# The second product of the up projection in five pairs: matmuls of 512 and 256 columns in place of three of 256

## The chip, the cores and the metric

The kernel runs on one core of one Trainium2 chip, in one launch. The metric is the time of that launch on the device, in microseconds; of several runs the median is taken. TensorE, VectorE, ScalarE and GpSimd are called PE, DVE, ACT and POOL in the rows of the profile; PEld is TensorE's weight load, SP is SyncE, from which most DMAs are issued.

## The reference

One block of a decoder on 512 tokens of 2048 channels in float32: an input projection that feeds two token mixers, an output projection, and a gated MLP with a causal convolution of width 3. The change touches the MLP's up projection alone:

```python
def _conv_ffn(h, w_up, conv_w, conv_b, w_down):
    u = h @ w_up                                   # (512, 2048) @ (2048, 11264)
    up = jnp.pad(u, ((0, 0), (CONV_WIDTH - 1, 0), (0, 0)))
    y = conv_b
    for j in range(CONV_WIDTH):
        y = y + conv_w[j] * up[:, j:j + T]
    val, gate = jnp.split(y, 2, axis=-1)
    return (jax.nn.silu(gate) * val) @ w_down
```

The 11264 columns of w_up are 44 blocks of 128 for the value and 44 for the gate.

## The kernel before, in words

**Precision by splitting.** TensorE multiplies in a short form of float32. To keep the precision, each operand is split in two: a high part (ScalarE casts it, L1387) and a low part (VectorE subtracts the high part from the original, L1388). A product then is three matmuls per block of 128 rows of the weights (mm3, L133 to L137): high weights by high activations, high weights by low activations, low weights by high activations. In the up projection each of them streams 256 columns, that is, half of the tokens, since a Strassen-like scheme works on halves.

**The mixed form.** The output projection's halves (out_half, L1301) use another helper, mm2 (L1216 to L1218). There the high and the low activations lie in one operand of two runs of 256 columns, and one matmul of 512 columns takes high weights by both; it fills the whole of a PSUM bank, one half from each. A second matmul of 256 columns adds low weights by high activations to the first half. Whoever reads the bank has to add its two halves.

**A pair.** The up projection walks over 44 pairs, each of a value block and a gate block (the loop is at L1614). A pair of 2 × 2 quarters of weights times 2 × 2 quarters of activations takes seven products instead of eight. Each product has eight weight blocks (8 × 128 rows), so 24 matmuls in mm3's form. In the order of the program these are: w11·Y11 into bank pa (copied to cap by ScalarE, L1633), the last product of the pair before (w22·T4), **w12·Y21 into bank pb**, then r1·T1, r2·T2, r4·Y22 and r3·T3. The r are sums of weight quarters, made on VectorE (r2 at L1649, r4 at L1657) or by DMAs that add on the way (r1, r3). After the product of w12, VectorE adds the bank to cap and writes the first half of u1 (L1639); u1 goes into the convolution (L1470, L1471) once its second half is there (L1659).

**The order of the work.** order at L1611 mixes pairs 10 to 19 with pairs 0 to 9: place 0 is pair 10, place 1 is pair 0, place 2 is pair 11, and so on up to place 19; places 20 to 43 are pairs 20 to 43. For pairs 0 to 9 the first two products were made earlier (first_two, L1409) and stored. Where each engine's instructions stand is decided by a scheduler when the kernel is built; each engine then runs its own in that order. The split weights (tile uw) have three buffers, so splits run ahead of TensorE by up to two products. Banks come from a pool of eight (L1204), each taken whole even where half of it is used.

Of the kernel before, what the change touches and what calls it, by code (L numbers as in the profile page):

```python
# [16 lines left out]
P = 128  # L17
T = 512
# [7 lines left out]
WC = 512  # L26
NWF = 8
NSLOT = 10
NB = 10
NA = 4  # L30
WARB = 5
# [36 lines left out]
def block_kernel(ctx, tc, a, out, stop=None, dbg=None):  # L68
    nc = tc.nc
    V, S, G, PE = nc.vector, nc.scalar, nc.gpsimd, nc.tensor  # L70
# [62 lines left out]
    def mm3(ps, wh, wl, xh, xl, start, stop, more=False, hold=False):  # L133

        muls = [lambda: PE.matmul(ps, wh, xh, start=start, stop=False, skip_group_check=more),  # L135
                lambda: PE.matmul(ps, wh, xl, start=False, stop=False, skip_group_check=more),  # L136
                lambda: PE.matmul(ps, wl, xh, start=False, stop=stop, skip_group_check=more)]  # L137
        if hold:
            late.extend(muls)
            return None  # L140
        if late:
            ins = muls[0]()
            for m in (late.pop(0), muls[1], late.pop(0), muls[2], late.pop(0)):
                with tc.issue_after(ins.ins):
                    ins = m()
            return ins
        for m in muls:
            ins = m()
        return ins
# [772 lines left out]
    def btile(tag="pb"):  # L922

        return psa.tile([P, 2, T], F32, tag=tag, name=tag)
# [263 lines left out]
    pb, py = btile(), btile("py")  # L1188
# [16 lines left out]
    HT = T // 2  # L1205
    H0, H1 = slice(0, HT), slice(HT, T)
    QW = 4 * P

    def bank():
        return psm.tile([P, T], F32, tag="b", name="b")  # L1210
# [5 lines left out]
    def mm2(ps, wh, wl, x, start, stop):  # L1216
        PE.matmul(ps[:, :].rearrange("p (a b) -> p a b", a=2), wh, x, start=start, stop=False)  # L1217
        PE.matmul(ps[:, 0:HT], wl, x[:, 0, :], start=False, stop=stop)  # L1218

    def wide(name):  # L1220

        return rb.tile([P, 4, HT], F32, tag="wide", name=name, bufs=3)
# [13 lines left out]
    def lay(pool, sizes):  # L1236
        for tag, n in sizes:
            pool.tile([P, n], F32, tag=tag, name="lay")
# [87 lines left out]
    Y11, Y21 = [None, None], [None, None]  # L1326
# [33 lines left out]
    ub = ctx.enter_context(tc.tile_pool(name="ub", bufs=1, side="right", reuse_waits="tile"))  # L1360
    lay(ub, [(f"s{i}", T) for i in range(NSLOT)])
    lay(ub, [(f"{t}{g}", 4 * T) for g in range(2) for t in ("t1", "t2", "t3", "y22")])
    lay(ub, [("w2", WS), ("edge", 72)])
    free += [(ub, f"s{i}") for i in range(NSLOT)]

# [15 lines left out]
    def wsplit(src, off=0):  # L1381
        n = src.shape[-1]
        i = nsplit[0] % 3
        nsplit[0] += 1
        w = (ea, ea, ub)[i].tile([P, WS], F32R, tag=f"w{i}", name="uw")
        hi, lo = w[:, off : off + n], w[:, 2 * QW + off : 2 * QW + off + n]
        S.copy(hi, src)  # L1387
        lo_of[0] = V.tensor_tensor(lo, src, hi.bitcast(F32), op=ALU.subtract)  # L1388
        return hi, lo

    def product(ps, w, Y, start=True):
        wh, wl = wsplit(w, 16)
        n = w.shape[-1] // P
        for k in range(n):
            sl = slice(k * P, (k + 1) * P)
            y = Y[k // 4]
            mm3(ps, wh[:, sl], wl[:, sl], y[:, 0, k % 4, :], y[:, 1, k % 4, :], start=start and k == 0,
                stop=k == n - 1, more=not start)

    def row(n, pool, tag):  # L1400
        t = pool.tile([P, 4 * QW], F32, tag=tag, name="wrow")
        nc.sync.dma_start(t, a["wup"][n, :, :])
        return t

    W1, W2 = slice(0, 2 * QW), slice(2 * QW, 4 * QW)
    T1, T2, T3, T4, Y22 = ([None, None] for _ in range(5))
    early = [tc.dram_tile([P, T], F32, name=f"early{n}") for n in range(NB)]

    def first_two(n):  # L1409

        w = row(2 * n, ea, f"t4{n % 2}")
        s_ = Slot("u1")
        ps = bank()[:, 0:HT]
        product(ps, w[:, W1], Y11)
        S.copy(s_[:, H1], ps)
        ps = bank()[:, 0:HT]
        product(ps, w[:, W2], Y21)
        V.tensor_add(s_[:, H0], s_[:, H1], ps)
        G.dma_start(early[n], s_.t)
        s_.done()  # L1420
# [3 lines left out]
    def combos():  # L1424
        for g in range(2):
            normed(g, H1, rstd)
            yield
            t = wide("t1")
            V.tensor_sub(t, x2q[g][:, :, H0], x2q[g][:, :, H1])
            T1[g] = split4(ub, f"t1{g}", t)  # L1430
            yield
            normed(g + 2, H1, rstd)
            yield
            t3 = wide("t3")
            V.tensor_sub(t3, x2q[g + 2][:, :, H1], x2q[g][:, :, H1])
            t2 = wide("t2")
            V.scalar_tensor_tensor(t2, t3, -1.0, x2q[g][:, :, H0], op0=ALU.mult, op1=ALU.subtract)
            yield
            T2[g] = split4(ub, f"t2{g}", t2)
            T3[g] = split4(ub, f"t3{g}", t3)  # L1440
            yield
            Y22[g] = split4(ub, f"y22{g}", x2q[g + 2][:, :, H1])
            V.scalar_tensor_tensor(t2, t2, -1.0, x2q[g + 2][:, :, H0], op0=ALU.mult, op1=ALU.subtract)
            t4.append(t2)
            yield

    steps = combos()
    for n in range(NB):
        first_two(n)
# [142 lines left out]
    def ahead_of_down(j):  # L1592
        if j == NF - 1:
            i = len(A1) // 2
            A1.extend(act_pair(i, *FIRST[i]))
# [3 lines left out]
    def last_product(p):  # L1599

        j, u1, u2, b, w22, x = p
        product(b, w22, T4, start=False)
        if x is None:
            S.copy(u2[:, H0], b)
        else:
            V.tensor_add(u2[:, H0], x[:, H0], b)
            x.done()
        finish_pair(j, u1, u2)


    order = [j for n in range(NB) for j in (NB + n, n)] + list(range(2 * NB, NF))  # L1611

    wq = [rb.tile([P, 4 * QW], F32, tag=f"x2_{i}", name="wquart") for i in (0, 2, 1, 3)]
    for n, j in enumerate(order):  # L1614
        wa, wb = wq[2 * (n % 2)], wq[2 * (n % 2) + 1]

        r1, w11, w12, w22 = wa[:, W1], wa[:, W2], wb[:, W1], wb[:, W2]
        nc.sync.dma_start(r1, a["wup"][2 * j + 1, :, W1])
        G.dma_start(r1, a["wup"][2 * j + 1, :, W2], accum_op=ALU.add)
        nc.sync.dma_start(w11, a["wup"][2 * j, :, W1])  # L1620
        nc.sync.dma_start(w12, a["wup"][2 * j, :, W2])
        nc.sync.dma_start(w22, a["wup"][2 * j + 1, :, W2])
        r3 = wide("r3").rearrange("p a b -> p (a b)")
        nc.sync.dma_start(r3, a["wup"][2 * j, :, W1])
        G.dma_start(r3, a["wup"][2 * j + 1, :, W1], accum_op=ALU.add)
        pa = bank()[:, 0:HT]
        cap = Slot("cap")
        if j < NB:
            u1 = Slot("u1")
            nc.sync.dma_start(u1.t, early[j])  # L1630
        else:
            product(pa, w11, Y11)
            S.copy(cap[:, H0], pa)  # L1633
            if pend:
                last_product(pend)
            u1 = Slot("u1")
            pb = bank()[:, 0:HT]
            product(pb, w12, Y21)
            V.tensor_add(u1[:, H0], cap[:, H0], pb)  # L1639
        ahead_of_down(j)  # L1640
        u2 = Slot("u2")
        pc = bank()[:, 0:HT]
        product(pc, r1, T1)
        S.copy(cap[:, H1], pc)
        if j < NB:
            last_product(pend)
        ahead_of_down(j)
        r2 = wide("r2").rearrange("p a b -> p (a b)")
        V.tensor_add(r2, r1, w11)  # L1649
        product(pa, r2, T2, start=j < NB)  # L1650
        if j < NB:
            V.tensor_add(cap[:, H0], u1[:, H1], pa)
        else:
            S.copy(cap[:, H0], pa)
        ahead_of_down(j)
        r4 = wide("r4").rearrange("p a b -> p (a b)")
        V.tensor_add(r4, r2, w12)  # L1657
        product(pc, r4, Y22, start=False)
        V.tensor_add(u1[:, H1], cap[:, H0], pc)  # L1659
        ahead_of_down(j)  # L1660
        if j < NB:
            pd = bank()[:, 0:HT]
            product(pd, r3, T3)
            V.tensor_add(u2[:, H1], cap[:, H0], cap[:, H1])
            V.tensor_add(u2[:, H1], u2[:, H1], pd)
            pend = (j, u1, u2, pd, w22, cap)
        else:
            product(pa, r3, T3, start=False)
            V.tensor_add(u2[:, H1], cap[:, H1], pa)
            cap.done()  # L1670
            pend = (j, u1, u2, pa, w22, None)
# [194 lines left out]
    for f in range(NWF):  # L1866
# [5 lines left out]
        ps = pss[f] if f < 4 else bank()  # L1872
# [11 lines left out]
    for f in range(NWF, KT):  # L1884
        n = f - NWF
# [107 lines left out]
```

## Time and profile before

| | |
|---|---|
| runs of the kernel before | 2160.95, 2161.58, 2162.29 us; median 2161.58 |
| the profiled execution | 2162.7 us, of which the span from the first to the last instruction is 2160.9 |
| mean granted TensorE clock | 0.992 of full speed |
| busy in the span | PE 98%, PEld 86%, DVE 78%, ACT 48%, POOL 11% |
| matmuls | 17864, with as many weight loads |
| up projection's pairs, 880.2 to 1650 us | PE 769.80 of 769.80 us, DVE 633.67, ACT 427.62, DMA share 0.82 |

A row of the view of instructions in order of time reads: start in us from the span's start, length in us, engine, line of the kernel, operation, what is written and read, shape, count, and in brackets the idle time before it and who ended it. Matmuls are pipelined: a recorded length of 0.28 us is the time through the pipeline, and the next matmul starts before that, so the cost of a matmul in a stream is the distance between two starts. A row of a stage's window gives, for each engine, the time in which it was busy and the number of instructions. In the groups of instructions the last columns are busy us, mean ns of one, and the engine's idle time just before them.

### The profile page before, as it was taken

The numbers are of one execution on the slowest core, as the hardware profiler recorded it, in microseconds if no ns is written. First come the engines' busy times: TensorE is split into PE (matmuls) and PEld (weight loads), VectorE is DVE, ScalarE is ACT, GpSimd is POOL, SyncE is SP. The second block draws the span as 40 slices with busy tenths as digits, with TensorE's granted clock in tenths as the row PEclk, the third lists the DMA queues.
The fourth block names the chain that finished last, engine by engine and source line by source line (L and its number), as shares of the span: only waits on it lengthen the run. The fifth ranks groups of instructions, "written<-read, shape, count | busy, mean of one in ns | idle before, by whom it ended". The sixth has DMA issues, their size and how long they took to land.

```text
span 2160.9 us, 44013 instructions
## 1 busy us (share of the span) xinstructions
PE 2110.9 (98%) x17864; PEld 1866.0 (86%) x17864; DVE 1678.0 (78%) x2615; ACT 1047.8 (48%) x1510; POOL 237.0 (11%) x376
## 2 busy tenths in 40 slices
PE   7999999999999999999999999999999999999997
PEld 3567777777767888999999999999999889987897
DVE  7998898988853678888888887777788657768764
ACT  4354444433433466555555555555556444443353
POOL 0002122221100101110110000000000000120000
PEclk9999999999999999999999999999999999999998
DMA  9976676656537565989888877777777635598764
GB/s 395 393 229 197 200 199 174 199 170 186 150 105 263 183 197 176 290 241 260 253 241 255 236 209 205 207 208 210 209 209 219 211 118 144 161 318 311 243 195 167
DMA packets 169485, 471.89 MB, mean 218 GB/s; under 512 B 21361, under 2 KB 29505, under 8 KB 159169
## 3 DMA queue, kind: packets, MB, share of 16 engines
q1 hardware_dynamic: 120370, 352.12, 48.1%
q0 software_dynamic: 27696, 79.20, 17.5%
q10 hardware_dynamic: 21216, 37.76, 5.7%
q8 instruction: 140, 2.29, 0.4%
q14 instruction: 63, 0.52, 0.1%
HBM read 432.81 MB, written 36.18 MB: 217 GB/s over the span
## 4 chain that ended last, share of the span: by engine, by line
PE 86%; DMA 5%; DVE 4%; ACT 2%; issue 2%; POOL 1%; POOLq 0%; ACTq 0%; DVEq 0%; SPq 0%
PE b L137 19%; PE b L135 19%; PE b L136 19%; PE mm L645 11%; PE pf L426 4%; PE b L1217 2%; PE b L1218 1%; DMA wrow<-wup 1%; PE pb L1047 1%; DVE war L764 1%; DMA wraw<-wout 1%; DMA wa<-ada 1%; PE pa L711 0%; ACT x L1317 0%; DMA wraw<-win 0%
## 5 line engine op out<-in xcount | busy, mean ns | idle before, releaser
L137 PE MATMUL b<-t,uw 128*128 128x256 f32 x1408 | 388.6, 276 | 0.0
L135 PE MATMUL b<-t,uw 128*128 128x256 f32 x1408 | 388.6, 276 | 0.0
L136 PE MATMUL b<-t,uw 128*128 128x256 f32 x1408 | 388.6, 276 | 0.0
L135 PE MATMUL b<-y,uw 128*128 128x256 f32 x1056 | 293.6, 278 | 4.1 <-ACT uw L1387 4.1
L137 PE MATMUL b<-y,uw 128*128 128x256 f32 x1056 | 292.8, 278 | 0.8 <-DVE uw L1388 0.7
L136 PE MATMUL b<-y,uw 128*128 128x256 f32 x1056 | 292.9, 277 | 0.0
L645 PE MATMUL mm<-ahl,whi 128*128 128x512 f32 x864 | 289.7, 409 | 2.1 <-DVE rk L548 1.4
L135 PEld LDWEIGHTS b<-t,uw 128*128 128x128 f32 x1408 | 264.3, 188 | 0.0
L136 PEld LDWEIGHTS b<-t,uw 128*128 128x128 f32 x1408 | 264.3, 188 | 0.0
L137 PEld LDWEIGHTS b<-t,uw 128*128 128x128 f32 x1408 | 264.3, 188 | 0.0
L1388 DVE TENSOR_TENSOR uw<-r,uw 128x1024 fp32r<-128x1024 f32 x164 | 200.6, 1224 | 76.7 <-ACT uw L1387 76.7
L1388 DVE TENSOR_TENSOR uw<-wquart,uw 128x1024 fp32r<-128x1024 f32 x156 | 190.9, 1224 | 68.0 <-ACT uw L1387 67.0
L1387 ACT CAST uw<-wquart 128x1024 fp32r<-128x1024 f32 x156 | 164.1, 1052 | 88.9 <-PE b L137 66.0
L135 PEld LDWEIGHTS b<-y,uw 128*128 128x128 f32 x1056 | 199.5, 189 | 4.8 <-ACT uw L1387 4.8
L137 PE MATMUL b<-act,uw 128*128 128x256 f32 (+1 forms) x608 | 200.5, 330 | 2.7 <-DVE uw L1388 2.7
L1388 DVE TENSOR_TENSOR uw<-wd,uw 128x1024 fp32r<-128x1024 f32 (+1 forms) x112 | 124.1, 1109 | 101.1 <-ACT uw L1387 100.3
L1387 ACT CAST uw<-r 128x1024 fp32r<-128x1024 f32 x164 | 172.5, 1052 | 60.6 <-PE b L137 60.6
L135 PE MATMUL b<-act,uw 128*128 128x256 f32 (+1 forms) x608 | 200.7, 330 | 0.0
L137 PEld LDWEIGHTS b<-y,uw 128*128 128x128 f32 x1056 | 199.5, 189 | 1.2 <-DVE uw L1388 1.2
L136 PE MATMUL b<-act,uw 128*128 128x256 f32 (+1 forms) x608 | 200.4, 330 | 0.0
L136 PEld LDWEIGHTS b<-y,uw 128*128 128x128 f32 x1056 | 199.6, 189 | 0.1
L645 PEld LDWEIGHTS mm<-ahl,whi 128*128 128x128 f32 x864 | 158.2, 188 | 43.2 <-issue 12.2
(356 smaller groups left out, 4601.2 us busy)
## 6 DMA issues: line engine op xcount, KB each, us to landing
wquart<-wup SPq DMA_DIRECT2D x176, 512.0 KB, 5.2
wa<-ada SPq DMA_DIRECT2D x48, 1024.0 KB, 9.1
war<-ada SPq DMA_DIRECT2D x192, 256.0 KB, 3.8
wd<-wdn SPq DMA_DIRECT2D x64, 512.0 KB, 4.1
wraw<-win ACTq DMA_DIRECT2D x118, 256.0 KB, 4.1
wraw<-wout SPq DMA_DIRECT2D x96, 256.0 KB, 3.5
wquart<-wup POOLq DMA_DIRECT2D x44, 512.0 KB, 6.8
r<-wup SPq DMA_DIRECT2D x44, 512.0 KB, 4.7
```

Of the source, the lines that this page charges most:

```text
L135: muls = [lambda: PE.matmul(ps, wh, xh, start=start, stop=False, skip_group_check=more), lambda: PE.matmul(ps, wh, xl, start=False, stop=F ...
L136: lambda: PE.matmul(ps, wh, xl, start=False, stop=False, skip_group_check=more),
L137: lambda: PE.matmul(ps, wl, xh, start=False, stop=stop, skip_group_check=more)]
L426: PE.matmul(pf[n % 2 * 4 + ii], w[:, sl], full[k], start=k == 0, stop=k == KT - 1)
L645: PE.matmul(ps, w[:, sl], x, start=first, stop=k == KT - 1 and i == 2)
L764: V.scalar_tensor_tensor(wa, wa, 1.0, cqs[kq], op0=ALU.mult, op1=ALU.mult, accum_out=modq[:, kq, j : j + 1])
L1047: PE.matmul(pt[HS[e], h, c * 2 * L : (c + 1) * 2 * L], nt[HS[e], s, :], rw[HS[e], s, :, :], start=True, stop=True)
L1217: PE.matmul(ps[:, :].rearrange("p (a b) -> p a b", a=2), wh, x, start=start, stop=False)
L1218: PE.matmul(ps[:, 0:HT], wl, x[:, 0, :], start=False, stop=stop)
L1387: S.copy(hi, src)
L1388: lo_of[0] = V.tensor_tensor(lo, src, hi.bitcast(F32), op=ALU.subtract)
```

## The change

At five places of the order (0, 2, 6, 14 and 28, all of them pairs whose first two products are made in the loop) the product w12·Y21 is made with mm2 in place of mm3: for each of the eight weight blocks one matmul of 512 columns, high weights by high and low activations, and one of 256 columns, low weights by high activations. The bank pb is used whole. VectorE then takes two additions in place of one: cap plus the second half of the bank, then that plus the first half. The split of the weights is the same.

```diff
+WIDE = (0, 2, 6, 14, 28)
...
+    def product_wide(ps, w, Y):
+        wh, wl = wsplit(w, 16)
+        for k in range(w.shape[-1] // P):
+            sl = slice(k * P, (k + 1) * P)
+            mm2(ps, wh[:, sl], wl[:, sl], Y[k // 4][:, :, k % 4, :], k == 0, k == 7)
...
             u1 = Slot("u1")
-            pb = bank()[:, 0:HT]
-            product(pb, w12, Y21)
-            V.tensor_add(u1[:, H0], cap[:, H0], pb)
+            pb = bank()
+            if n in WIDE:
+                product_wide(pb, w12, Y21)
+                V.tensor_add(u1[:, H0], cap[:, H0], pb[:, HT:T])
+                V.tensor_add(u1[:, H0], u1[:, H0], pb[:, 0:HT])
+            else:
+                product(pb[:, 0:HT], w12, Y21)
+                V.tensor_add(u1[:, H0], cap[:, H0], pb[:, 0:HT])
```

On PE, at place 0, the second half of the product (weight blocks five to eight, activations y3) was twelve matmuls in a row before; b_9864 is the bank, uw the split weights:

```order
L135 MATMUL b_9864<-y3_8974,uw_9865 128x256
L136 MATMUL b_9864<-y3_8974,uw_9865 128x256
L137 MATMUL b_9864<-y3_8974,uw_9865 128x256
L135 MATMUL b_9864<-y3_8974,uw_9865 128x256
L136 MATMUL b_9864<-y3_8974,uw_9865 128x256
L137 MATMUL b_9864<-y3_8974,uw_9865 128x256
L135 MATMUL b_9864<-y3_8974,uw_9865 128x256
L136 MATMUL b_9864<-y3_8974,uw_9865 128x256
L137 MATMUL b_9864<-y3_8974,uw_9865 128x256
L135 MATMUL b_9864<-y3_8974,uw_9865 128x256
L136 MATMUL b_9864<-y3_8974,uw_9865 128x256
L137 MATMUL b_9864<-y3_8974,uw_9865 128x256
```

Now it is eight, and behind them follows the next product, r1·T1:

```order
L1218 MATMUL b_9864<-y3_8974,uw_9865 128x512
L1219 MATMUL b_9864<-y3_8974,uw_9865 128x256
L1218 MATMUL b_9864<-y3_8974,uw_9865 128x512
L1219 MATMUL b_9864<-y3_8974,uw_9865 128x256
L1218 MATMUL b_9864<-y3_8974,uw_9865 128x512
L1219 MATMUL b_9864<-y3_8974,uw_9865 128x256
L1218 MATMUL b_9864<-y3_8974,uw_9865 128x512
L1219 MATMUL b_9864<-y3_8974,uw_9865 128x256
L136 MATMUL b_9887<-t10_9281,uw_9888 128x256
```

In each of the five products 24 matmuls became 16, and no other matmul changed its place.

On DVE, at place 2, the addition of the bank (L1639, b_10260) stood between the two steps of the convolution of the pair before (yg), and a split of r4 came right behind:

```order
L1388 TENSOR_TENSOR uw_10321<-r2_10319,uw_10321 128x1024
L1470 SCALAR_TENSOR_TENSOR yg_10249<-u2_10023,ncw_9775,yg_10249 128x511
L1639 TENSOR_TENSOR u1_10259<-cap_10191,b_10260 128x256
L1471 SCALAR_TENSOR_TENSOR yg_10249<-u2_10023,ncw_9775,yg_10249 128x510
L1388 TENSOR_TENSOR uw_10351<-r4_10349,uw_10351 128x1024
L1483 TENSOR_TENSOR yv_10248<-yv_10248,yg_10249 128x512
L1649 TENSOR_TENSOR r2_10488<-wquart_9823 128x1024
```

Now (line numbers are some higher; the addition is L1647, the convolution L1477 and L1478, the split L1389) it reads:

```order
L1389 TENSOR_TENSOR uw_10307<-r2_10305,uw_10307 128x1024
L1477 SCALAR_TENSOR_TENSOR yg_10242<-u2_10016,ncw_9775,yg_10242 128x511
L1647 TENSOR_TENSOR u1_10252<-cap_10184,b_10253 128x256
L1478 SCALAR_TENSOR_TENSOR yg_10242<-u2_10016,ncw_9775,yg_10242 128x510
L1648 TENSOR_TENSOR u1_10252<-u1_10252,b_10253 128x256
L1389 TENSOR_TENSOR uw_10337<-r4_10335,uw_10337 128x1024
L1490 TENSOR_TENSOR yv_10241<-yv_10241,yg_10242 128x512
L1661 TENSOR_TENSOR r2_10474<-wquart_9823 128x1024
```

The second addition, L1648, was put behind the convolution's second step and ahead of the split of r4. At places 6, 14 and 28 it stands the same way.

On DVE at place 0 there is no convolution of an earlier pair between them. Before, behind the combined weights r4:

```order
L1657 TENSOR_TENSOR r4_9953<-r2_9923,wquart_9822 128x1024
L1388 TENSOR_TENSOR uw_9925<-r2_9923,uw_9925 128x1024
L1639 TENSOR_TENSOR u1_9863<-cap_9834,b_9864 128x256
L1388 TENSOR_TENSOR uw_9955<-r4_9953,uw_9955 128x1024
L1649 TENSOR_TENSOR r2_10092<-wquart_9823 128x1024
L1388 TENSOR_TENSOR uw_9983<-r3_9830,uw_9983 128x1024
L1657 TENSOR_TENSOR r4_10122<-r2_10092,wquart_9824 128x1024
```

And now:

```order
L1669 TENSOR_TENSOR r4_9946<-r2_9916,wquart_9822 128x1024
L1389 TENSOR_TENSOR uw_9918<-r2_9916,uw_9918 128x1024
L1647 TENSOR_TENSOR u1_9863<-cap_9834,b_9864 128x256
L1648 TENSOR_TENSOR u1_9863<-u1_9863,b_9864 128x256
L1389 TENSOR_TENSOR uw_9948<-r4_9946,uw_9948 128x1024
L1661 TENSOR_TENSOR r2_10085<-wquart_9823 128x1024
L1389 TENSOR_TENSOR uw_9976<-r3_9830,uw_9976 128x1024
L1669 TENSOR_TENSOR r4_10115<-r2_10085,wquart_9824 128x1024
```

Here both additions follow each other, and the split of r4 stands behind them. Nothing else on DVE moved, and on ACT, POOL and SP the order is as it was.

## The prediction

> **What bounds the kernel now.** I read the page first, then the windows of the stages that use the two matmul forms, then the waits of TensorE inside the up projection, and last single instructions in order of time.
>
> From the page of the kernel before:
>
> ```profile
> span 2160.9 us, 44013 instructions
> ...
> PE 2110.9 (98%) x17864; PEld 1866.0 (86%) x17864; DVE 1678.0 (78%) x2615; ACT 1047.8 (48%) x1510; POOL 237.0 (11%) x376
> ...
> PE 86%; DMA 5%; DVE 4%; ACT 2%; issue 2%; POOL 1%; POOLq 0%; ACTq 0%; DVEq 0%; SPq 0%
> ```
>
> TensorE carries the end: 86% of the chain that ended last is PE. The windows say how this looks in two stages: the output projection's halves (735 to 828 us), where the mixed form of 512 and 256 columns runs already, and the up projection from its last stop nearly to its end (880.2 to 1650).
>
> ```profile
> core 0: us, PE busy (x) PEld busy (x) DVE busy (x) ACT busy (x) POOL busy (x), PEclk, DMA share, GB/s
> 735.00:828.00 93.00, 91.52 (x519) 78.88 (x518) 69.88 (x119) 56.37 (x100) 8.68 (x16) 1.00 0.61 189
> 880.20:1650.00 769.80, 769.80 (x6795) 769.80 (x6794) 633.67 (x736) 427.62 (x557) 77.12 (x90) 1.00 0.82 227
> ```
>
> In the up projection PE is busy for all of 769.80 us, at a granted clock of 1.00, while VectorE works 633.67 us, 82%. The list of TensorE's waits for that window has no entry. 769.80 us over 6795 matmuls is 113.3 ns from one to the next. So in the stage that the change touches, time is the number of matmuls times their spacing, and anything else counts only if it makes PE stop.
>
> **The change, part by part.**
>
> *TensorE.* A product has eight weight blocks. Before, each block is three matmuls of 256 columns; this is the second product of the pair at place 2 of the order:
>
> ```profile
> 928.60 0.28 PE L135 MATMUL b<-y,uw 128*128 128x256 f32 x1
> 928.71 0.28 PE L136 MATMUL b<-y,uw 128*128 128x256 f32 x1
> 928.83 0.28 PE L137 MATMUL b<-y,uw 128*128 128x256 f32 x1
> 928.94 0.28 PE L135 MATMUL b<-y,uw 128*128 128x256 f32 x1
> ...
> 931.21 0.28 PE L137 MATMUL b<-y,uw 128*128 128x256 f32 x1
> 931.32 0.28 PE L135 MATMUL b<-t,uw 128*128 128x256 f32 x1
> ```
>
> One block takes 928.94 − 928.60 = 0.34 us, the product 931.32 − 928.60 = 2.72 us. The recorded 0.28 us is the length of one pipelined matmul and overlaps the next; only start to start counts.
>
> After, each block is one matmul of 512 columns and one of 256. The columns streamed are the same: 3 × 256 = 512 + 256 = 768. What a column costs in a long matmul shows in the down projection, where the operand's 512 columns lie next to each other:
>
> ```profile
> 1700.06 0.39 PE L136 MATMUL b<-act,uw 128*128 128x512 f32 x1
> 1700.29 0.39 PE L137 MATMUL b<-act,uw 128*128 128x512 f32 x1
> 1700.51 0.39 PE L135 MATMUL b<-act,uw 128*128 128x512 f32 x1
> 1700.74 0.39 PE L136 MATMUL b<-act,uw 128*128 128x512 f32 x1
> ```
>
> Three steps take 0.68 us, so 0.227 us each: exactly twice 0.1133. There is no visible fixed part per matmul that eight fewer instructions could save. By this row a wide block costs 0.227 + 0.113 = 0.340 us, and the change is worth 0.
>
> The Trainium skill, page "TensorE: Matmul & The Clock Gate", section "Back-to-back issue gap", gives N/2.4 + 2.5 ns as the spacing on a warm clock, so each matmul saved would return about 2.5 ns. By that rule (an estimate) the 8 × 5 = 40 matmuls saved give 0.1 us back; the trace's 227 against 2 × 113.3 ns shows no such part.
>
> The nearest row, however, is the same helper in the same form, with the operand in two runs of 256 columns: the output projection's halves.
>
> ```profile
> 760.09 0.28 PE L1218 MATMUL b<-ahl,wlo 128*128 128x256 f32 x1
> ...
> 761.96 0.40 PE L1217 MATMUL b<-ahl,whi 128*128 128x512 f32 x1
> 762.21 0.28 PE L1218 MATMUL b<-ahl,wlo 128*128 128x256 f32 x1
> 762.33 0.40 PE L1217 MATMUL b<-ahl,whi 128*128 128x512 f32 x1
> 762.56 0.28 PE L1218 MATMUL b<-ahl,wlo 128*128 128x256 f32 x1
> ```
>
> From 760.09 to 762.56 lie seven blocks: 2.47 / 7 = 0.353 us, which is 0.013 us more than three short matmuls. The dearest block there is 761.96 to 762.33, 0.37 us. I take 0.353, since form, operand layout and clock are those of the change: 5 products × 8 blocks × 0.013 us = +0.52 us. The ends are 0 (by the contiguous row) and 40 × 0.03 = +1.2 us (by the dearest block).
>
> *VectorE.* Five products get one more addition of 256 columns out of the bank. Its price is the group of the addition that stands there now:
>
> ```profile
> L1639 DVE TENSOR_TENSOR u<-cap,b 128x256 f32<-128x256 f32 x33 | 13.7, 416 | 0.1
> ```
>
> 5 × 0.416 = 2.08 us on VectorE. It waits for the first addition. Queued behind it on VectorE are a split of weights (for the third product from there), then the conv's product and the next combined weights; PE needs the split's low part at the first matmul that takes low weights, the third of its product. VectorE at place 2 of the order, and PE at that third matmul:
>
> ```profile
> 931.69 0.42 DVE L1639 TENSOR_TENSOR u<-cap,b 128x256 f32<-128x256 f32 x1
> 932.02 0.75 DVE L1471 SCALAR_TENSOR_TENSOR yg<-u,ncw,yg 128x510 f32<-128x510 f32 x1
> 932.68 1.22 DVE L1388 TENSOR_TENSOR uw<-r,uw 128x1024 fp32r<-128x1024 f32 x1
> ...
> 938.31 1.22 DVE L1388 TENSOR_TENSOR uw<-wquart,uw 128x1024 fp32r<-128x1024 f32 x1 [0.23 <-ACT uw L1387]
> ```
>
> ```profile
> 936.99 0.28 PE L137 MATMUL b<-y,uw 128*128 128x256 f32 x1
> ```
>
> The split ends at 932.68 + 1.22 = 933.90 and its first use is at 936.99: 3.09 us ahead. The addition takes at most 0.42 us of that; 2.67 us are left. VectorE's queue is short of work again at 938.31, where it stood idle for 0.23 us. At place 0, where no conv of an earlier pair is in between:
>
> ```profile
> 898.88 0.42 DVE L1639 TENSOR_TENSOR u<-cap,b 128x256 f32<-128x256 f32 x1
> 900.01 1.23 DVE L1388 TENSOR_TENSOR uw<-r,uw 128x1024 fp32r<-128x1024 f32 x1 [0.70 <-ACT uw L1387]
> ```
>
> ```profile
> 904.35 0.28 PE L137 MATMUL b<-y,uw 128*128 128x256 f32 x1
> ```
>
> Here the idle 0.70 us ahead of the split swallows the addition, and the split is 904.35 − 901.24 = 3.11 us early anyway. So the additions cost the path nothing; if nothing hid them, 2.1 us.
>
> *What else moves.* ScalarE's, SyncE's and GpSimd's instructions stand in the same order as before, and so do PE's products. The bank of the second product is given back one addition later; the pool has eight banks, and PE waits for none in the window. The half of u1 is finished about 0.4 us later; its next writer and the conv come only after three more products, 3 × 2.72 = 8 us on. No DMA moves.
>
> *Sum.* +0.52 us (TensorE) + 0 (VectorE). The profiled execution took 2162.7 us, of which 2160.9 are its span; it would become 2163.2. The median of the runs shown, 2161.58, becomes 2162.1. A change of 0.2%, 4.3 us, is about what a measurement of this kernel can tell from none; the forecast is an eighth of it.
>
> **The rivals.**
>
> *Weight loads are the limit (faster).* In the window PEld is busy for 769.80 of 769.80 us, one load for each matmul. If a load were what sets 113.3 ns, a wide product would pay 16 loads in place of 24, and 8 × 113.3 ns = 0.91 us would go, 4.5 us over five: 2157.1 us. Against it: with one load per 512 columns the spacing is 227 ns, so columns, not loads, set it there, and half as many columns need the same 113.3; and in the output projection, where PEld is busy 78.88 of 93.00 us, the mixed form gained nothing. The Trainium skill, page "Perfetto Trace Analysis", section "Identifying the Most-Contended Engine", takes the busy share of the weight loads as a good measure of how near TensorE is to its limit, and under "Optimizing Tensor Performance" calls larger matmuls more efficient where possible; both speak for this rival, and the two rows of spacing speak against it. Chance 3 in 100.
>
> *A stop that costs the clock (slower).* If VectorE's longer queue made PE stop for some 3 us, the clock would go too. It happens once, just ahead of the pairs:
>
> ```profile
> 870.17 0.28 PE L137 MATMUL b<-y,uw 128*128 128x256 f32 x1
> 873.48 0.58 PE L135 MATMUL b<-y,uw 128*128 128x256 f32 x1 [3.04 <-ACT uw L1387]
> 875.02 0.41 PE L137 MATMUL b<-y,uw 128*128 128x256 f32 x1
> 875.23 0.41 PE L135 MATMUL b<-y,uw 128*128 128x256 f32 x1
> 880.07 0.28 PE L136 MATMUL b<-y,uw 128*128 128x256 f32 x1
> ```
>
> After a stop of 3.2 us the matmuls stand 0.21 us apart until 880.07, some 31 of them with 0.1 us extra: 3.2 + 3.1 = 6.3 us for one such stop, 2168.4 with the TensorE term. Its place is pair 0, whose split follows the addition at once. It decides from the point where a split comes about 6 us late (3.1 us ahead plus 3 us of stop); the addition makes it 0.42. Chance 3 in 100; 1 more for a slowing of the long matmuls beyond all rows here.
>
> *The additions lie open.* 0.52 + 2.08 = 2.6 us, 2164.2: still within 0.2%. Chance 2.
>
> That the change does not do what it says is excluded by the order: 16 matmuls stand for 24 in five products, and nothing else is new but five additions.
>
> **How the numbers follow.** The forecast, 2162.1, has 91 in 100. The four executions shown lie between 2160.95 and 2162.7, so I allow 1.75 us of scatter to each side: the low end is the median with a TensorE term of 0, 2161.58 − 1.75 = 2159.8; the high end takes the dearest block, 2161.58 + 1.2 + 1.75 = 2164.5, which holds most of the case with open additions. Faster by over 0.2% is the first rival, 0.03. Slower is the second and the unknown, 0.04. Within 0.2% is the rest, 0.93.
>
> **What would show it.** Right: in the profile after, the two lines of mm2 have 40 more matmuls each, on b<-y; a wide block stands 0.34 to 0.37 us from the next; the product takes 2.72 to 2.95 us; the window of the up projection still has no TensorE wait; five additions of about 0.42 us follow. Wrong: wide blocks at clearly less than 0.34 us (then loads or a fixed part counted), TensorE waits for a low split behind the new addition, or a granted clock under 1.00 in the stage.

## The result, and the profile after

The changed kernel takes 2192.52 us (median of four runs, 2189.7 to 2195.33); the kernel before took 2161.26 beside it (four runs, 2159.28 to 2162.29). The ratio is 1.0146, 95% interval 1.0128 to 1.0163: 31.3 us slower, where 0.5 us was forecast and the dearest rival stood at 2168.4 us. The ratios in this document leave out executions more than 1.5% above the fastest of the same kernel; since executions of some of these kernels, the one before among them, turned out to fall into two groups about 30 us apart, the groups are listed beside the ratios.

From the page of the kernel after, with the groups of TensorE's matmuls and weight loads (busy us, mean ns of one):

```profile
span 2189.9 us, 43943 instructions
PE 2139.5 (98%) x17824; PEld 1893.2 (86%) x17824; DVE 1682.5 (77%) x2620; ACT 1045.8 (48%) x1510; POOL 236.3 (11%) x376
...
L138 PE MATMUL b<-t,uw 128*128 128x256 f32 x1408 | 395.6, 281 | 0.0
...
L136 PEld LDWEIGHTS b<-t,uw 128*128 128x128 f32 x1408 | 270.3, 192 | 0.3
L137 PEld LDWEIGHTS b<-t,uw 128*128 128x128 f32 x1408 | 264.3, 188 | 0.0
```

The same groups on the page of before:

```profile
L137 PE MATMUL b<-t,uw 128*128 128x256 f32 x1408 | 388.6, 276 | 0.0
...
L135 PEld LDWEIGHTS b<-t,uw 128*128 128x128 f32 x1408 | 264.3, 188 | 0.0
```

There are 40 fewer matmuls and PE is busy 28.6 us longer. The group b<-t belongs to the products that the change does not touch, and yet each of these matmuls is recorded 5 ns longer, and one of the three weight loads of a block 4 ns longer. So the time is not at the five places. The windows from behind place 0's product to nearly the end of the pairs, after:

```profile
897.00:1650.00 753.00, 753.00 (x6364) 751.51 (x6363) 599.89 (x698) 401.19 (x523) 71.63 (x82) 1.00 0.80 219
```

and before:

```profile
897.00:1650.00 753.00, 753.00 (x6647) 753.00 (x6646) 618.71 (x721) 417.89 (x545) 73.59 (x85) 1.00 0.82 227
```

Both are full, at a granted clock of 1.00, but in the same time 283 fewer matmuls pass. Before, one comes every 753 / 6647 = 113.3 ns. After, four wide products lie in the window, 64 matmuls in 32 blocks of 0.353 us (below), 11.3 us; the other 741.7 us hold 6300 narrow ones, 117.7 ns each. Single instructions in order of time, after, at place 0, show where it begins:

```profile
893.57 0.28 PE L138 MATMUL b<-y,uw 128*128 128x256 f32 x1
...
893.91 0.28 PE L138 MATMUL b<-y,uw 128*128 128x256 f32 x1
894.02 0.39 PE L1218 MATMUL b<-y,uw 128*128 128x512 f32 x1
894.25 0.28 PE L1219 MATMUL b<-y,uw 128*128 128x256 f32 x1
894.37 0.40 PE L1218 MATMUL b<-y,uw 128*128 128x512 f32 x1
...
896.84 0.28 PE L136 MATMUL b<-t,uw 128*128 128x256 f32 x1
...
897.19 0.28 PE L136 MATMUL b<-t,uw 128*128 128x256 f32 x1
...
1702.44 0.40 PE L136 MATMUL b<-act,uw 128*128 128x512 f32 x1
...
1703.42 0.50 PE L138 MATMUL b<-act,uw 128*128 128x512 f32 x1 [0.35 <-DVE uw L1389]
```

Ahead of the first wide block three narrow matmuls take 893.91 − 893.57 = 0.34 us. A wide block takes 894.37 − 894.02 = 0.35 us, and from 894.02 to 896.84 eight take 2.82 us, 0.353 each, as it was priced. Behind it three narrow ones take 897.19 − 896.84 = 0.35 us too, and so it goes on to the end of the pairs. The next stop of PE is at 1703.42. I call the two spacings the 340 rhythm and the 353 rhythm, after the nanoseconds per three narrow matmuls (113.3 and 117.8 each), read more finely from the starts over hundreds of them.

The sum: 1702.44 − 896.84 = 805.6 us, less 11.3 us for four wide products, is 794.3 us or some 6740 narrow matmuls at 117.8 ns. Times 4.45 ns that is 30.0 us, and the five wide products add 5 × 8 × 0.013 = 0.5: 30.5 us of the measured 31.3. (The spans of the two profiled executions differ by 29.0 us: the one after came to place 0 1.9 us sooner, at 894.02 against 895.96.) In the down projection the two kernels are alike again. A window of 140 us of its narrow matmuls, in before:

```profile
1765.00:1905.00 140.00, 140.00 (x1238) 140.00 (x1237) 106.35 (x104) 64.28 (x85) 21.61 (x32) 1.00 0.57 162
```

and in after:

```profile
1793.50:1933.50 140.00, 140.00 (x1238) 140.00 (x1237) 107.44 (x106) 65.17 (x87) 22.50 (x34) 1.00 0.58 163
```

### The profile page after: what moved, and what is told of

Same layout as the page of the kernel before. It is cut to its first block, busy times and chain, and to the rows that moved or that the text cites. A ratio compares the mean times of both kernels' runs of the same rounds, so it can differ in the third digit from the quotient of the medians.

```text
span 2189.9 us, 43943 instructions
## 1 busy us (share of the span) xinstructions
PE 2139.5 (98%) x17824; PEld 1893.2 (86%) x17824; DVE 1682.5 (77%) x2620; ACT 1045.8 (48%) x1510; POOL 236.3 (11%) x376
## 4 chain that ended last, share of the span: by engine, by line
PE 87%; DVE 4%; DMA 4%; ACT 2%; issue 2%; POOL 1%; POOLq 0%; DVEq 0%; ACTq 0%
PE b L137 19%; PE b L138 19%; PE b L136 19%; PE mm L646 11%; PE pf L427 4%; PE b L1218 3%; PE b L1219 1%; DMA wrow<-wup 1%; PE pb L1048 1%; DVE war L765 1%; PE pa L712 1%; DMA wa<-ada 1%; ACT x L1318 0%; DMA wraw<-win 0%; PE pf L136 0%
## 5 line engine op out<-in xcount | busy, mean ns | idle before, releaser
L138 PE MATMUL b<-t,uw 128*128 128x256 f32 x1408 | 395.6, 281 | 0.0
L137 PE MATMUL b<-t,uw 128*128 128x256 f32 x1408 | 395.6, 281 | 0.0
L136 PE MATMUL b<-t,uw 128*128 128x256 f32 x1408 | 395.6, 281 | 0.0
L136 PE MATMUL b<-y,uw 128*128 128x256 f32 x1016 | 286.7, 282 | 4.4 <-ACT uw L1388 4.4
L138 PE MATMUL b<-y,uw 128*128 128x256 f32 x1016 | 285.7, 281 | 0.8 <-DVE uw L1389 0.7
L137 PE MATMUL b<-y,uw 128*128 128x256 f32 x1016 | 285.9, 281 | 0.0
L1389 DVE TENSOR_TENSOR uw<-r,uw 128x1024 fp32r<-128x1024 f32 x164 | 200.4, 1223 | 81.8 <-ACT uw L1388 81.2
L1389 DVE TENSOR_TENSOR uw<-wquart,uw 128x1024 fp32r<-128x1024 f32 x156 | 190.8, 1224 | 82.9 <-ACT uw L1388 82.9
L1389 DVE TENSOR_TENSOR uw<-wd,uw 128x1024 fp32r<-128x1024 f32 (+1 forms) x112 | 123.9, 1107 | 100.4 <-ACT uw L1388 100.4
L136 PEld LDWEIGHTS b<-y,uw 128*128 128x128 f32 x1016 | 195.6, 192 | 5.1 <-ACT uw L1388 5.1
L138 PEld LDWEIGHTS b<-y,uw 128*128 128x128 f32 x1016 | 191.7, 189 | 1.2 <-DVE uw L1389 1.2
L137 PEld LDWEIGHTS b<-y,uw 128*128 128x128 f32 x1016 | 192.1, 189 | 0.1
```

## The experiments

Three theories stood at the start. **A:** the wide product tips TensorE's stream into the 353 rhythm, which then keeps itself until something else tips it back; the price is set by how far it is to there. **B:** each wide product is dear by itself, some 6.2 us. **C:** it is the use of both halves of the bank and the second addition, not the lengths of the matmuls. Executions of the kernel before ran beside the experiments in each session. They fell into two groups:

| session | low group | between | high group |
|---|---|---|---|
| first four experiments | 15, 2154.9 to 2162.57 | 1 at 2168.62 | 15, 2185.59 to 2196.33 |
| two passes, kicks | 10, 2156.06 to 2165.92 | | 3, 2187.59 to 2191.4 |
| the other two-pass kernels, offset 0, thin kick | 18, 2156.15 to 2166.72 | | 7, 2184.13 to 2194.38 |
| offsets; what tips | 1, 2157.94 | | 1, 2192.91 |

So the code of before takes about 2161 us in 44 of 71 executions and about 2190 in 26.

### One wide product, the first

```diff
-WIDE = (0, 2, 6, 14, 28)
+WIDE = (0,)
```

> Only place 0 is wide. Theory A (rhythm): the first wide product tips TensorE's stream from 113.3 ns per matmul of 256 columns to 117.8, and it stays there until TensorE next stops, at the start of the down projection; one wide product then costs as much as five: about 2192 us. Theory B (dear products): each of the five wide products costs by itself a fifth of the 31 us, 6.2 us, here about 2167.5 us. Theory C (the two halves of the bank, or the added additions on VectorE, slow TensorE near them): also about 2167.5 us.

Ten executions took 2185.71 to 2194.47, median 2189.01 (ratio 1.0075, 1.0025 to 1.0124, against a before that fell into both groups; the median of its low group beside these experiments is 2160.87, 28.1 us less). The window of this kernel:

```profile
897.00:1650.00 753.00, 753.00 (x6396) 753.00 (x6395) 599.86 (x697) 402.28 (x525) 71.61 (x82) 1.00 0.80 218
```

753 / 6396 = 117.7 ns with no wide product in the window. One does what five do: B falls.

### One wide product, the last

```diff
-WIDE = (0, 2, 6, 14, 28)
+WIDE = (28,)
```

> Only place 28 is wide. Theory A: the slow rhythm begins only there, at about 1377 us of 1673, so some 2600 matmuls pay 4.45 ns each: +11.6 us, about 2173 us, with 113.3 ns ahead of the place and 117.8 ns behind it. Theories B and C: 6.2 us, about 2167.5 us, as with the first alone.

Eight executions took 2167.47 to 2176.25, two 2189.3 and 2191.43; the median of all ten is 2173.1 (ratio 1.0067, 1.0029 to 1.0105), that of the eight 2171.59, 10.7 us above before's low group. The windows ahead of and behind the product (1374.6 to 1377.5) in the profiled execution, of 2176.25 us:

```profile
897.00:1370.00 473.00, 473.00 (x4176) 473.00 (x4175) 398.46 (x472) 263.00 (x338) 48.93 (x56) 1.00 0.86 239
1380.00:1650.00 270.00, 270.00 (x2294) 270.00 (x2294) 206.45 (x233) 142.77 (x191) 24.21 (x28) 1.00 0.74 199
```

473 / 4176 = 113.3 ns ahead, 270 / 2294 = 117.7 behind. It lasts until PE's next stop near 1685: 307 us, some 2610 matmuls, 11.6 us. That is A's price by position. The product itself takes 2.82 us, as at place 0, and 2.72 before: B falls once more. The two executions near 2190 lie where before's high group lies; they left no trace that shows their rhythm ahead of the product.

### Both halves of the bank, with short matmuls

```diff
-            mm2(ps, wh[:, sl], wl[:, sl], Y[k // 4][:, :, k % 4, :], k == 0, k == 7)
+            y = Y[k // 4]
+            PE.matmul(ps[:, 0:HT], wh[:, sl], y[:, 0, k % 4, :], start=k == 0, stop=False)
+            PE.matmul(ps[:, HT:T], wh[:, sl], y[:, 1, k % 4, :], start=False, stop=False, skip_group_check=True)
+            PE.matmul(ps[:, 0:HT], wl[:, sl], y[:, 0, k % 4, :], start=False, stop=k == 7)
```

> All five places use both halves of the bank and both additions, but with three matmuls of 256 columns in place of 512 and 256. Theory A, with the 512 columns as what tips the stream: 113.3 ns throughout, about 2161 to 2162 us. Theory C: the slowdown stays, about 2192 us.

Five executions took 2158.26 to 2162.86 and five 2187.75 to 2196.19: the two groups of before, in the same shares (ratio 0.9984, 0.9915 to 1.0053). C falls: with halves and additions, but without the long matmuls, the kernel behaves as before. The profiled execution, 2196.19 us, shows that the 353 rhythm can begin without any changed product, some 30 us ahead of place 0, behind a wait of PE of 0.68 us that ended at 862.4. Two starts that lie three matmuls apart:

```profile
862.63 0.28 PE L136 MATMUL b<-y,uw 128*128 128x256 f32 x1
...
862.99 0.28 PE L136 MATMUL b<-y,uw 128*128 128x256 f32 x1
```

and the window of the pairs:

```profile
900.00:1650.00 750.00, 750.00 (x6370) 750.00 (x6370) 599.28 (x698) 399.16 (x520) 71.62 (x82) 1.00 0.80 219
```

862.99 − 862.63 = 0.36 us for three, and 750 / 6370 = 117.7 ns in the pairs.

### The 512 columns in one run

```diff
-        t = pool.tile([P, 2, 4, HT], F32R, tag=tag, name=tag)
+        if tag in ("y2", "y3"):
+            t = pool.tile([P, 4, 2, HT], F32R, tag=tag, name=tag).rearrange("p k h t -> p h k t")
+        else:
+            t = pool.tile([P, 2, 4, HT], F32R, tag=tag, name=tag)
```

> All five places wide, but the high and low parts of Y21 are stored next to each other for each weight block, so that the 512 columns are one run in memory and not two runs 4 KB apart. If the two runs are what costs and tips the stream: a wide block takes 0.340 us, 113.3 ns behind it, about 2161 us. If the change of lengths (512, 256, 512, ...) alone tips it: 0.353 us for a block and about 2192 us.

All ten executions took 2185.99 to 2193.91, median 2190.48 (ratio 1.0106, 1.0064 to 1.0147, against the same two groups of before). The window behind place 0's product:

```profile
897.50:1650.00 752.50, 752.50 (x6360) 751.01 (x6359) 599.84 (x698) 400.81 (x523) 71.63 (x82) 1.00 0.80 219
```

Behind it, with the four wide products taken off as above, 741.2 us / 6296 = 117.7 ns. That the operand lies in two runs is not the cause.

### The lengths in two passes

All eight matmuls of 512 columns come first, then all eight of 256: at the five places, at place 0 alone, and at all 34 pairs whose second product is made in the loop.

```diff
-        for k in range(w.shape[-1] // P):
-            sl = slice(k * P, (k + 1) * P)
-            mm2(ps, wh[:, sl], wl[:, sl], Y[k // 4][:, :, k % 4, :], k == 0, k == 7)
+        for k in range(8):
+            PE.matmul(ps[:, :].rearrange("p (a b) -> p a b", a=2), wh[:, k * P : (k + 1) * P],
+                      Y[k // 4][:, :, k % 4, :], start=k == 0, stop=False)
+        for k in range(8):
+            PE.matmul(ps[:, 0:HT], wl[:, k * P : (k + 1) * P], Y[k // 4][:, 0, k % 4, :], start=False, stop=k == 7)
```

> The five wide places with all eight matmuls of 512 columns first and the eight of 256 behind them. If taking turns between 512 and 256 is what tips the stream: the eight 512s stand 227 ns apart, the 256s 113.3, and the executions lie near 2161 us, or fall in two groups as those of the kernel before do. If any matmul of 512 columns in two runs tips it: 2190 us in all executions.

> Two passes (eight 512s, then eight 256s) at place 0 alone, all else as before. If two passes set the fast rhythm, as at place 0 of the run with five, one of them is enough, since TensorE does not stop behind it: all executions near 2158 us. If they leave the rhythm as they find it, two groups near 2160 and 2190 us.

> Two passes at all 34 places that make the product in the loop. Theory A: the rhythm is fast from place 0, nothing more is to be had from it; 29 further products pay 8 x 234 + 8 x 113.3 ns = 2.78 us in place of 2.72, about +1.7 us, near 2160 us. If each wide product gained time by itself, the more the better: below 2155.

| two passes at | median of ten | from, to | ratio, 95% |
|---|---|---|---|
| the five places | 2158.1 | 2157.14, 2167.79 | 0.9987, 0.9954 to 1.002 |
| place 0 | 2163.08 | 2156.86, 2167.09 | 0.999, 0.9959 to 1.002 |
| 34 places | 2159.93 | 2156.62, 2165.47 | 0.9969, 0.9931 to 1.0007 |

Not one of the 30 executions is in the high group. The same matmuls and the same additions, in another order, cost nothing: what tips the stream in the change is that the two lengths take turns. The profiled execution with five places came to place 0 in the 353 rhythm and left it in the other. The last three narrow matmuls ahead of the product (from 890.14 on), the two passes, and the first matmul behind:

```profile
890.14 0.28 PE L136 MATMUL b<-y,uw 128*128 128x256 f32 x1
...
890.50 2.03 PE L1404 MATMUL b<-y,uw 128*128 128x512 f32 x8
892.37 1.07 PE L1407 MATMUL b<-y,uw 128*128 128x256 f32 x8
893.28 0.28 PE L136 MATMUL b<-t,uw 128*128 128x256 f32 x1
```

and the window from there:

```profile
893.00:1650.00 757.00, 757.00 (x6648) 755.57 (x6648) 623.23 (x729) 419.65 (x547) 74.24 (x85) 1.00 0.83 225
```

The three ahead take 0.36 us. The eight long ones stand (892.37 − 890.50) / 8 = 0.234 us apart, twice 117 ns; the eight short ones (893.28 − 892.37) / 8 = 0.114. The switch lies at the seam of the two passes, and it holds: with the 32 matmuls that four more such products save, 757.00 us / 6680 = 113.3 ns. The profiled executions of the other two kernels came to place 0 in the 340 rhythm already, and none of their two-pass products, 34 of them in one kernel, tipped it.

### The change with thin matmuls behind it

The change as it was, and behind r1·T1 at each of the five places four matmuls of 2 columns into a bank that nobody reads (the thin kick):

```diff
-        product(pc, r1, T1)
+        last, wk = product(pc, r1, T1)
+        if n in WIDE:
+            sp = bank()
+            for i in range(4):
+                with tc.issue_after(last.ins):
+                    last = PE.matmul(sp[:, 0:2], wk, Y11[0][:, 0, 0, 0:2], start=True, stop=True)
```

> The change as it is, and one product later (behind r1 T1) four matmuls of 2 columns into an unused bank, as at the two places where these brought 340 ns back. Theory A: the wide products themselves cost 5 x 0.1 us, one slow product each 5 x 0.1 us, the kicks some 5 x 0.5 us: near 2161 to 2164 us in all executions, with 340 ns between the kick and the next wide place. Theory B (dear products): 2192 us.

Ten executions took 2159.13 to 2167.14, median 2161.92 (ratio 0.9991, 0.9962 to 1.0019). At place 0, behind the last wide block (894.90) and on both sides of the four thin matmuls:

```profile
894.90 0.28 PE L136 MATMUL b<-t,uw 128*128 128x256 f32 x1
...
895.25 0.28 PE L136 MATMUL b<-t,uw 128*128 128x256 f32 x1
...
897.72 0.50 PE L1661 MATMUL b<-y,uw 128*128 128x2 f32 x4
...
898.29 0.28 PE L137 MATMUL b<-t,uw 128*128 128x256 f32 x1
...
898.63 0.28 PE L137 MATMUL b<-t,uw 128*128 128x256 f32 x1
```

The rows are three matmuls apart: 0.35 us between the wide product and the thin ones (895.25 − 894.90), 0.34 behind them (898.63 − 898.29). With the rhythm set back within 3 us, the wide products cost what the prediction said, next to nothing. The same happens at the other four places in this trace. So the 31 us are paid by the matmuls behind them.

### What sets the rhythm back, and what tips it

Two kernels, each profiled once. In the first, wide products of alternating lengths at sixteen places, and between them, behind the second product, one disturbance each; in the second the same with two-pass products, so that most disturbances meet the 340 rhythm. They are extra matmuls of the columns named, into a bank that is not read, or a matmul of one column that reads a copy made by ScalarE and was meant to make PE wait ("stop").

```diff
-WIDE = (0, 2, 6, 14, 28)
+WIDE = (0, 4, 8, 12, 16, 20, 22, 24, 26, 28, 30, 32, 34, 36, 38, 40)
...
-                product(pb[:, 0:HT], w12, Y21)
+                last, wk = product(pb[:, 0:HT], w12, Y21)
+                if n in KICK:
+                    kick(*KICK[n], last, wk, pb, cap)
```

> A look at what ends the slow rhythm. Wide products stand at 16 places (0, 4, 8, 12, 16, 20, 22, 24 and every second place to 40), and between them, behind the narrow second product of another place, something extra into a bank that nobody reads: one, two or three matmuls of 512 columns in one run (places 2, 6, 23, 31, 33), a matmul of one column that waits for ScalarE (a stop of TensorE; 10, 25, 37), matmuls of 2 columns (14, 27, 35), of 256 (18, 21), 384 (29) or 64 (39, 41). Theory A, in the form that a rhythm lasts until something else comes: each wide product ends in 353 ns per three matmuls, and behind at least the stops, perhaps behind the 512s, 340 ns return until the next wide one. If only a long pause as that ahead of the pairs can end it, all stays at 353. If the pitch follows from what is near in place or time (Theory C), it is 340 between the wide products whatever stands there.

> The counterpart of the run with kicks: the wide products at the same 16 places are made in two passes, which so far left the fast rhythm behind them, and between them stand extra matmuls into an unused bank: 512 columns in one run (1, 2, 3, 1 of them at places 2, 6, 21, 23), a wait for ScalarE (10, 25), 2 columns (14, 27, 35), 256 (18), 384 (29), 64 (39, 41), and 512 and 256 in turn, once, twice and eight times, with one set of weights (31, 33, 37). If only taking turns tips the stream: 353 ns per three behind places 31, 33 and 37 up to the next wide place, 340 everywhere else. If any matmul of another length, or any stop, lets the rhythm fall anew: 353 ns behind several of the others as well.

| disturbance | met the 353 rhythm: 340 behind it | met the 340 rhythm: 353 behind it |
|---|---|---|
| 512 columns, once | 0 of 2 | 2 of 2 |
| 512, twice | 2 of 2 | |
| 512, three times | 1 of 3 | |
| 512 and 256 in turn, once or twice | | 2 of 2 |
| 512 and 256 in turn, eight times | 0 of 1 | |
| 384, once | 1 of 1 | 0 of 1 |
| 256, once or three times | 0 of 3 | |
| 64, once | 0 of 1 | 1 of 1 |
| 64, four times | 1 of 1 | 0 of 1 |
| 2 columns, once | 0 of 1 | 1 of 1 |
| 2 columns, four times | 2 of 2 | 2 of 2 |
| one column, behind a copy ("stop") | 0 of 4 | 0 of 1 |
| product of 512s, then 256s | 7 of 12 | 0 of 4 |

The first kernel took 2189.34 us; each of its sixteen alternating products left the 353 rhythm behind it. The second took 2185.99. One matmul of 512 columns in the stream of the second is enough; the rows but the long one are three matmuls apart:

```profile
929.11 0.28 PE L139 MATMUL b<-y,uw 128*128 128x256 f32 x1
...
929.45 0.39 PE L1421 MATMUL b<-y,uw 128*128 128x512 f32 x1
929.68 0.28 PE L139 MATMUL b<-t,uw 128*128 128x256 f32 x1
...
930.03 0.28 PE L139 MATMUL b<-t,uw 128*128 128x256 f32 x1
```

Ahead of it three take 0.34 us, behind it 0.35. So it is not the one form of the change that tips: many odd matmuls throw the stream from either rhythm into the other. Two things found before are limited by the second kernel. Two passes do not always set the stream back (7 of 12, although they never tipped it), and the four thin matmuls that restored it in the two kernels before tip it in this one. No rule of size or count orders the table.

The five "stops" were none. In both traces the list of TensorE's waits in the pairs is empty, and the matmul of one column starts 0.18 or 0.19 us behind the narrow one before it, where narrow ones stand 0.11 to 0.12 apart. Whether a stop changes the rhythm has to be read where PE does wait, ahead of the pairs. In the second kernel (rows three apart ahead of the stop, the stop, and rows three apart well behind it):

```profile
868.79 0.28 PE L141 MATMUL b<-y,uw 128*128 128x256 f32 x1
...
869.13 0.28 PE L141 MATMUL b<-y,uw 128*128 128x256 f32 x1
872.18 0.38 PE L139 MATMUL b<-y,uw 128*128 128x256 f32 x1 [2.78 <-ACT uw L1391]
...
890.14 0.28 PE L139 MATMUL b<-y,uw 128*128 128x256 f32 x1
...
890.49 0.28 PE L139 MATMUL b<-y,uw 128*128 128x256 f32 x1
```

Three take 0.34 us ahead of the stop and 0.35 behind it, up to place 0. Of the thirteen traces in which the weights start at 16 there, eight leave the stops ahead of the pairs in the 340 rhythm and five in the 353. Two of these five lost it again ahead of place 0, where one or two matmuls came about 0.1 us late and nothing was inserted (in the two-pass kernel with 34 places, the step from 883.02 to 883.22). The other three came to place 0 in it: the kernel with halves of 256, in which no odd matmul follows and which took 2196.19 us, and two kernels whose two passes at place 0 ended it. So a high execution of before is probably one that leaves these stops in the 353 rhythm and meets nothing that ends it; its own high executions left no trace.

### Where the weights start in their buffer

wsplit puts the high part 16 elements into its buffer and the low part 16 behind its middle. The change with both at 0, in the narrow and the wide products alike:

```diff
-        wh, wl = wsplit(w, 16)
+        wh, wl = wsplit(w, 0)
```

> The change as it is (five places, 512 and 256 in turn), but the split weights start at the buffer's first element and not at element 16, in all narrow and wide products. If the two rhythms come of where the weights lie against the activations in memory, another start changes the pitches (not 340.0 and 353.3 ns per three) or which of them lasts. If they do not depend on it: 353.3 behind place 0, near 2190 us.

Four executions took 2209.76 to 2215.8, median 2215.04 (ratio 1.0196, 1.012 to 1.0271). Each matmul now takes 120.0 ns, ahead of place 0 too. Two starts with ten matmuls between them:

```profile
950.67 0.28 PE L136 MATMUL b<-t,uw 128*128 128x256 f32 x1
...
951.99 0.28 PE L138 MATMUL b<-t,uw 128*128 128x256 f32 x1
```

and a group of weight loads from 900 to 1650 us:

```profile
L138 PEld LDWEIGHTS b<-t,uw 128*128 128x128 f32 x1280 | 245.7, 192 | 0.0
```

Eleven steps take 1.32 us, 0.120 each. The loads of the other two lines are recorded at 192 ns as well; in the 353 rhythm it is one of three, in the 340 rhythm none. The next kernel is before's, without wide products, with other starts of high and low part at places 20 to 39:

```diff
-        hi, lo = w[:, off : off + n], w[:, 2 * QW + off : 2 * QW + off + n]
+        o = PLACES.get(at[0], (off, off)) if off else (0, 0)
+        hi, lo = w[:, o[0] : o[0] + n], w[:, 2 * QW + o[1] : 2 * QW + o[1] + n]
```

> The kernel before, with the start of the high and of the low weights in their buffer changed from place to place behind place 20: high at 0, 1, 2, 4, 8, 12, 14 or 16 elements and low at as much or more (16 and 16 is the kernel before). If where the weights start sets which rhythms there are: 120.0 ns per matmul at (0, 0), as in the run with offset 0, other pitches at other pairs of starts, and 113.3 or 117.8 at (16, 16). If only the buffer as a whole matters: one pitch for all places.

It took 2178.51 us, before beside it 2157.94. By the starts, (high, low), over 120 matmuls inside each place: (0, 0) 120.0 ns; (8, 12) and (8, 16) 118.9 and 118.8; (0, 8), (4, 4), (8, 8), (12, 12) and (1, 1) 118.3; (0, 4), (0, 16), (4, 8), (4, 12), (4, 16) and (0, 2) 117.8; (2, 16) 116.7; (2, 2) 115.6; the other three tried lie between 116.9 and 118.7, and only (16, 16) has 113.3. It came back to that at place 34 and at places 40 to 43 with no stop between; here at place 34, which begins at 1494.23. Rows three matmuls apart:

```profile
1493.87 0.28 PE L138 MATMUL b<-t,uw 128*128 128x256 f32 x1
...
1494.23 0.28 PE L138 MATMUL b<-y,uw 128*128 128x256 f32 x1
...
1494.58 0.28 PE L138 MATMUL b<-y,uw 128*128 128x256 f32 x1
...
1494.92 0.28 PE L138 MATMUL b<-y,uw 128*128 128x256 f32 x1
```

0.36 us, then 0.35 across the first block, then 0.34. It is one execution, so another rhythm may be had at some of these starts too. But how far apart matmuls of one shape stand thus depends on where the weights lie, at one and the same clock.

## Why the prediction was wrong, by its own steps

**The step that failed** is the first: "time is the number of matmuls times their spacing, and anything else counts only if it makes PE stop". The spacing, 769.80 us over 6795 matmuls, was taken for a property of the instruction. It is a state of the stream, and the change moved the stream into another one. The sum had a term for the 80 matmuls at the five places and none for the some 6740 behind them; 4.45 ns on each is 30.0 us.

**The price of a wide block** was right by itself: 0.353 us. But the row that it was taken from said more than the prediction read in it. 0.353 us per 768 columns, in whichever form, is what the 353 rhythm gives. And narrow matmuls in that rhythm stood in the trace of before, just ahead of the stage:

```profile
849.09 0.28 PE L135 MATMUL b<-y,uw 128*128 128x256 f32 x1
...
849.44 0.28 PE L135 MATMUL b<-y,uw 128*128 128x256 f32 x1
```

These two are three matmuls apart: 0.35 us, at the same shape. Had they been set beside the 0.34 us of the pairs, a rival would have followed: the product leaves the stream at 0.353 per block until the next stop, some 6750 × 4.5 ns = 30 us.

**The additions** cost the path nothing, as forecast. Their groups in the kernel after:

```profile
L1647 DVE TENSOR_TENSOR u<-cap,b 128x256 f32<-128x256 f32 x5 | 2.1, 416 | 0.2 <-PE b L1219 0.2
L1648 DVE TENSOR_TENSOR u<-u,b 128x256 f32<-128x256 f32 x5 | 2.1, 415 | 0.0
```

and the whole list of TensorE's waits from 880 to 1720 us there is one entry, in the down projection:

```profile
PE b L138 <- DVE uw L1389: 0.4, 1, 0.4
```

The kernel before has the same one there, of 0.3 us.

**The rivals.** No stop and no loss of clock appeared (1.00 throughout), so the slow rival had the right sign for a wrong reason, and none of the rivals held the mechanism that came. Weight loads as the limit that fewer loads would relieve: against it, 272 fewer loads in the two-pass kernel with 34 places gained nothing beyond its interval. But where the weights lie does set the spacing, so loads bear on it in another way than the rival had it.

The prediction used the Trainium skill's N/2.4 + 2.5 ns ("TensorE: Matmul & The Clock Gate", "Back-to-back issue gap"), which that section gives for a single isolated matmul; worked out from it, an estimate, 256 columns take 109 ns. These runs show 113.3, 117.8 and 120.0 where it has one figure. The same section of the Trainium skill says that in a stream of loads and matmuls both set the spacing; the experiment with the starts is in keeping with that, since only the place of the weights changed there and the spacing went from 113.3 to as much as 120.0 ns. The busy share of the weight loads, which the Trainium skill's page "Perfetto Trace Analysis" ("Identifying the Most-Contended Engine") takes as a measure of how near TensorE is to its limit, does not tell the two rhythms apart here: 753.00 of 753.00 us in the windows of before and of the kernel with one wide product at place 0 alike.

**What the list of signs lacked.** It named the wide blocks, waits and the clock, and on each of them the prediction came out right. It did not name the spacing of the matmuls that nobody touched.

**Settled:** the loss is the 353 rhythm behind the first wide product (one product costs it all, the last one 11.6 us, the thin kick takes it away); in the change it is the turns of the two lengths that bring it about (the same matmuls in two passes do not), not bank, additions or the operand's two runs. **Open:** what in the chip holds a rhythm; why a stop leaves the stream now in one rhythm and now in the other, and whether that alone makes the 26 high executions of before; why one odd matmul flips the stream and another does not. That the recorded loads lengthen by 4 ns with the rhythm, and that it follows the weights' place, makes their reading a candidate, which is argued and not shown.

**A better version.** Two passes, or the thin kick, hold the low group's time in all of 40 executions; against before's low group none of them is measurably faster. What they may gain is the high group: 26 of 71 executions × 29 us is some 11 us on average. The kernel that showed two passes failing to set the rhythm back in 5 of 12 places warns against counting on it.

## What to carry to other kernels

Where an engine is full and waits for nothing, compare the spacing of the instructions that a change does not touch, ahead of and behind the first place that it does touch; a few nanoseconds on thousands of them outweigh the whole of what was edited. Two spacings for one shape in the trace before, or executions in two groups, mean that the spacing is a state: then price an odd instruction in the stream by the distance to the next event that resets it. Three runs that agree do not show that a kernel has one time: here the first four of before agreed within 0.2%, and over a third of 71 lay 29 us higher.

## What the runs showed of the hardware

At a granted clock of 1.00, matmuls of 256 columns stood 113.3, 117.8 or 120.0 ns apart, and at some other starts of the weights between 115.6 and 118.9; 512 columns took twice 113 or twice 117. A rhythm held for over 800 us and some 6700 matmuls. One matmul of 2, 64 or 512 columns ended the 340 rhythm in the middle of a stream, and a stop of 2.78 us ahead of the pairs was left in another rhythm than it was met in. Moving the weights by 16 elements of 4 bytes made the changed kernel 22.5 us slower still (2215.04 against 2192.52, in two sessions).
